# Attention in a two-layer backbone: two of five key blocks are split in two parts by POOL from an SBUF copy, three by DVE from PSUM

## The chip, the cores and the metric

One core of one Trainium2 chip runs the whole program in one launch. The metric is the device time of an execution in microseconds, the median of the runs shown. TensorE is called PE here (PEld is its weight load), VectorE DVE, ScalarE ACT, GpSimd POOL and SyncE SP.

## What is computed

The program is a two-layer backbone over 1024 latent tokens and 256 context tokens, width 1024. Layer 0 mixes with grouped-query attention (12 query heads, 4 key heads, head size 64) beside a convolution, layer 1 with a long convolution beside a recurrence; each layer ends in a gated feed-forward block. The change lies in the attention of layer 0 alone:

```python
def block_attention(q, k, v):                       # per block of 128 queries
    s = jnp.einsum('bqhgd,bkhd->bhgqk', q_blk, k)   # scores
    p = jax.nn.softmax(s, axis=-1)
    return jnp.einsum('bhgqk,bkhd->bqhgd', p, v)
# latent queries see 256 context keys and 1024 latent keys; context queries see the 256 context keys
```

## The kernel before

**Units.** `attention_all` (L875) walks 60 units. A latent unit is one head and 256 latent queries against all 1280 keys; there are 48 (4 key heads, 3 query heads each, 4 times 256 queries). A context unit is one head and the 256 context queries against 256 keys; there are 12. Each unit has two halves of 128 queries.

**Scores.** `score_steps` (L998) multiplies queries by keys into the one PSUM tile `S`, which holds both halves (L1008, L1009: two matmuls per piece, because the keys lie there in two parts). For each half DVE finds the negated row maximum `nm` (L1025) and ACT writes the exponentials `p` to SBUF and their sum `sm` (L1026).

**Values.** `value_steps` (L1030) turns the exponentials round. For each block of 256 keys, five per latent unit (`b` from 0 to 4) and one per context unit, PE makes four 128x128 transposes into a PSUM tile `pT` of 128x512 (L1048). There are two buffers for it (`npt=2`), and the transposes `zT` of the next head's queries and keys (L993) use the same two. The matmul with the values takes each factor as a sum of two parts of a shorter type: ACT rounds `pT` to the high part `ph` (L1052), DVE subtracts, `pl = pT - ph` (L1053), and both stay in SBUF. The buffer of `pT` is free when DVE has read it. The matmuls that add `ph` and `pl` into the PSUM tile `o` (L1059) are put off by `DELAY = 2` blocks (`late`). At a unit's end ACT copies one half of `o` to `bot` (L1067), DVE adds it and multiplies by the reciprocal sum (two instructions `ot`, by the helper `add`, L1188), and SP stores `ot`. `o` has one buffer, so the next unit's first matmul into it waits for the second `ot`.

**Beside it.** Two side streams are fed in. `stack_gen` (L960) prepares the next key head: POOL and ACT split queries and keys in two parts `zst` (L981 to L986), in batches of two or four tiles, PE transposes them, ACT copies the results. `load_early` (L825) reads finished pieces of the attention output back from DRAM as `ysrc` (two buffers), and POOL splits them, `och` (L833) and `ocl` (L834 by the helper). Near the end POOL also splits the first weights of the next stage, `wlo` (L332).

**Order.** The order on each engine comes from a scheduler, which sorts by the priority of the program's order and by its own estimate of when an instruction is ready. On the chip each engine then runs its list strictly in that order, and waits where an operand is not there.

Of the kernel before, what the change touches and what calls it, by code (L numbers as in the profile page):

```python
# [10 lines left out]
F32 = mybir.dt.float32  # L11
F32R = mybir.dt.float32r
AF = mybir.ActivationFunctionType
ALU = mybir.AluOpType
# [3 lines left out]
P = 128  # L18
# [229 lines left out]
class Kern:  # L248
# [781 lines left out]
    def value_steps(self, u, state):  # L1030

        nc = self.nc
        ab = self.ab
        nk, r, oq, h0 = u
        vs = self.gr[h0 // 3][3]
        ob = self.pa.tile([P, 512], F32, name="o", tag="o", bufs=1)
        o = ob[:, :256]
        nb = nk // 256
        rs = ab.tile([P, 2], F32, name="rs", tag="rs", bufs=2)
        nc.vector.reciprocal(out=rs, in_=state["sm"])  # L1040
        for b in range(nb):
            pt = self.pa.tile([P, 512], F32, name="pT", tag="pt", bufs=self.npt)
            for a in range(2):
                for i, p in enumerate(state["p"]):
                    kc = 2 * b + a
                    if nb > 1 and i == 0:
                        kc = (kc - 2) % NT
                    nc.tensor.transpose(pt[:, (2 * a + i) * P:(2 * a + i + 1) * P], p[:, kc * P:(kc + 1) * P],  # L1048
                                        self.ident)
            ph = ab.tile([P, 512], F32R, name="ph", tag="ph", bufs=4)  # L1050
            pl = self.st.tile([P, 512], F32R, name="pl", tag="sq", bufs=3)
            nc.scalar.copy(ph, pt)  # L1052
            nc.vector.tensor_tensor(out=pl, in0=pt, in1=ph.bitcast(F32), op=ALU.subtract)  # L1053

            def then(b=b, ph=ph, pl=pl):
                for a in range(2):
                    kc = 2 * b + a
                    for j, x in enumerate((ph, pl)):
                        nc.tensor.matmul(o, lhsT=vs[:, kc], rhs=x[:, a * 256:a * 256 + 256],  # L1059
                                         start=(kc == 0 and j == 0), stop=(kc == nk // P - 1 and j == 1))  # L1060
                if b < nb - 1:
                    return
                bot, ot = (ab.tile([64, 256], F32, name=m, tag=m, bufs=n) for m, n in (("bot", 1), ("ot", 2)))
                rt = ob[:64, 256:512]
                for i in range(2):
                    nc.tensor.transpose(rt[:, i * P:(i + 1) * P], rs[:, i:i + 1].to_broadcast([P, 64]), self.ident)
                nc.scalar.copy(bot, o[64:128])  # L1067
                self.add(ot, o[0:64], bot)
                self.add(ot, rt, ot, ALU.mult)
                h = h0 + r  # L1070
                nc.sync.dma_start(out=self.od[h // 2][(h % 2) * 64:(h % 2) * 64 + 64, oq:oq + 256], in_=ot)
            self.late.append(then)
            if len(self.late) > self.DELAY:
                self.late.pop(0)()
            yield
# [874 lines left out]
```

## Time and profile before

| | |
|---|---|
| runs | 3852.33, 3854.68, 3864.87 us; median 3854.68 |
| profiled execution | 3860.75 us, its span 3858.7 us, so 2.05 us lie around the span |
| PE busy | 3516.5 us, 91% of the span |
| DVE, ACT, POOL busy | 2289.8 (59%), 1248.0 (32%), 1334.2 us (35%) |
| attention | some 418 to 1001 us of the span |

The span runs from the first to the last instruction. "Busy" counts instructions in progress; a matmul's end is modelled, and consecutive ones overlap. A group of instructions is one line of code on one engine with one shape: its count, total and mean time, and the idle time of the engine just before them with what ended it. The chain that ended last is followed back from the end of a window, at each step to what released an instruction or to the one before it on its engine; "issue" in it is time in which the engine waited for nothing that the profile shows.

### The profile page before, as it was taken

What the parts mean: (1) busy time and instruction counts of PE and PEld (TensorE: products, weight loads), DVE (VectorE), ACT (ScalarE), POOL (GpSimd) and SP (SyncE); (2) the same over time, 40 slices, a digit from 0 to 9 for tenths busy, and PEclk for the clock granted to TensorE, in tenths of its full rate; (3) what the DMA queues carried; (4) which work ended last, traced back from release to release, by engine and by line L of the source; (5) the groups of instructions that cost most, each with busy time, mean ns of one, the idle gap of its engine ahead of it and who ended that gap; (6) DMA issues with size and microseconds to landing.
All of it is one profiled execution on the core that took longest, in us unless ns stands there. A gap on an engine that the chain in (4) does not pass through costs nothing.

```text
span 3858.7 us, 47940 instructions
## 1 busy us (share of the span) xinstructions
PE 3516.5 (91%) x18708; PEld 2924.3 (76%) x18708; DVE 2289.8 (59%) x2847; ACT 1248.0 (32%) x2123; POOL 1334.2 (35%) x1003
## 2 busy tenths in 40 slices
PE   7988688888899999999999899999878899999998
PEld 4768466776687888888888778977666778888886
DVE  5977456666326666655555689455698554343435
ACT  4135566666333211122222422222112342222222
POOL 3248331100152111123333554355566642222223
PEclk9999789999999999999999899999898999999999
DMA  5376111000223223212222367433345311111111
GB/s 204 118 189 142 59 60 33 21 19 25 101 71 99 77 93 106 73 54 72 81 77 72 120 199 208 140 98 96 117 147 195 129 58 49 45 48 50 44 50 55
DMA packets 204017, 356.39 MB, mean 92 GB/s; under 512 B 23632, under 2 KB 124560, under 8 KB 203792
## 3 DMA queue, kind: packets, MB, share of 16 engines
q1 hardware_dynamic: 172240, 311.22, 24.8%
q0 software_dynamic: 27648, 35.76, 4.4%
q10 hardware_dynamic: 3904, 6.36, 0.5%
q8 instruction: 148, 2.42, 0.3%
q14 instruction: 77, 0.63, 0.1%
HBM read 275.04 MB, written 62.39 MB: 87 GB/s over the span
## 4 chain that ended last, share of the span: by engine, by line
PE 65%; DVE 12%; issue 4%; ACT 3%; DMA 3%; POOL 1%; SPq 0%; POOLq 0%; ACTq 0%; DVEq 0%
PE dl L338 13%; PE dl L339 13%; PE dl L340 13%; PE pj L338 2%; PE pT L1048 2%; PE pj L339 2%; PE pj L340 2%; DVE nm L1025 2%; PE o L1059 2%; DVE pl L1053 2%; PE S L1008 1%; PE dc L338 1%; PE dc L340 1%; PE dc L339 1%; PE S L1009 1%
## 5 line engine op out<-in xcount | busy, mean ns | idle before, releaser
L332 POOL TENSOR_TENSOR wlo<-wraw,whi 128x1024 fp32r<-128x1024 f32 (+1 forms) x226 | 567.4, 2516 | 1289.0 <-ACT whi L331 1288.8
L339 PE MATMUL dl<-hl,whi 128*128 128x512 f32 x1920 | 763.2, 398 | 3.8 <-POOL hl L1188 2.9
L338 PE MATMUL dl<-hh,whi 128*128 128x512 f32 x1536 | 607.0, 396 | 11.9 <-DVE fc L1099 8.7
L340 PE MATMUL dl<-hh,wlo 128*128 128x512 f32 x1536 | 607.9, 396 | 0.0
L331 ACT CAST whi<-wraw 128x1024 fp32r<-128x1024 f32 (+1 forms) x226 | 225.1, 1005 | 887.3 <-PE dl L339 415.2
L339 PEld LDWEIGHTS dl<-hl,whi 128*128 128x128 f32 x1920 | 362.9, 189 | 88.2 <-POOL hl L1188 4.6
L338 PEld LDWEIGHTS dl<-hh,whi 128*128 128x128 f32 x1536 | 289.3, 188 | 80.7 <-issue 7.0
L1097 DVE SCALAR_TENSOR_TENSOR fc<-dl,cols,fc 128x1023 f32<-128x1023 f32 x84 | 107.4, 1279 | 408.6 <-ACT fc L1096 408.6
L340 PEld LDWEIGHTS dl<-hh,wlo 128*128 128x128 f32 x1536 | 289.3, 188 | 68.7
L872 DVE SCALAR_TENSOR_TENSOR x<-dl,modT,x 128x1024 f32<-128x1024 f32 x160 | 204.1, 1277 | 113.7 <-PE dl L340 112.2
L338 PE MATMUL dl<-gs,whi 128*128 128x512 f32 x640 | 253.2, 396 | 9.1 <-DVE fc L1099 9.1
L339 PE MATMUL dl<-gs,whi 128*128 128x512 f32 x640 | 250.2, 391 | 0.0
L340 PE MATMUL dl<-gs,wlo 128*128 128x512 f32 x640 | 250.0, 391 | 0.0
L1053 DVE TENSOR_TENSOR pl<-pT,ph 128x512 fp32r<-128x512 f32 x252 | 167.5, 685 | 65.9 <-ACT ph L1052 65.3
L1048 PE MATMUL pT<-ident,p 128*128 128x128 f32 x1008 | 166.8, 288 | 41.6 <-DVE pl L1053 34.5
L1052 ACT CAST ph<-pT 128x512 fp32r<-128x512 f32 x252 | 142.7, 587 | 153.5 <-PE pT L1048 152.2
L1025 DVE TENSOR_REDUCE nm<-S 128x1 f32<-128x1280 f32 (+1 forms) x120 | 153.0, 1275 | 51.5 <-PE S L1009 47.1
L1059 PE MATMUL o<-ph,vs 128*128 128x256 f32 x504 | 147.0, 305 | 36.9 <-ACT ph L1052 18.9
L1048 PEld LDWEIGHTS pT<-ident,p 128*128 128x128 f32 x1008 | 121.5, 146 | 64.4 <-DVE pl L1053 48.4
L1192 DVE SCALAR_TENSOR_TENSOR conv<-u,cols,conv 128x1287 f32<-128x1287 f32 (+14 forms) x96 | 160.4, 1698 | 0.9
L338 PE MATMUL dl<-hl,whi 128*128 128x512 f32 x384 | 155.0, 405 | 1.7 <-ACT whi L331 0.8
L1059 PE MATMUL o<-pl,vs 128*128 128x256 f32 x504 | 152.3, 325 | 2.2 <-DVE pl L1053 2.2
(373 smaller groups left out, 8390.9 us busy)
## 6 DMA issues: line engine op xcount, KB each, us to landing
wraw<-in_wup SPq DMA_DIRECT2D x88, 512.0 KB, 3.5
adaw<-in_adaw SPq DMA_DIRECT2D x128, 256.0 KB, 2.8
wraw<-in_wdn SPq DMA_DIRECT2D x44, 512.0 KB, 3.5
adaw<-in_adaw SPq DMA_DIRECT2D x32, 512.0 KB, 4.1
df<-in_dftf POOLq DMA_DIRECT2D x64, 256.0 KB, 3.8
wraw<-in_w1f SPq DMA_DIRECT2D x24, 512.0 KB, 3.7
x<-in_xT SPq DMA_DIRECT2D x16, 640.0 KB, 10.1
spd<-so SPq DMA_DIRECT2D x68, 128.0 KB, 2.2
```

Source lines behind the costliest of these rows:

```text
L331: nc.scalar.copy(hi[:, :cols], raw[:, :cols])
L332: nc.gpsimd.tensor_tensor(out=lo[:, :cols], in0=raw[:, :cols], in1=hi[:, :cols].bitcast(F32), op=ALU.subtract)
L338: mm(out, lhsT=lh, rhs=rh, start=first, stop=False)
L339: mm(out, lhsT=lh, rhs=rl, start=False, stop=False)
L340: mm(out, lhsT=ll, rhs=rh, start=False, stop=last)
L872: nc.vector.scalar_tensor_tensor(out=xl, in0=pl, scalar=self.mod(l, j, m, 0), in1=xl, op0=ALU.mult, op1=ALU.add)
L1025: nc.vector.tensor_reduce(out=nm[:, i:i + 1], in_=s, op=ALU.max, axis=AX.X, negate=True)
L1048: nc.tensor.transpose(pt[:, (2 * a + i) * P:(2 * a + i + 1) * P], p[:, kc * P:(kc + 1) * P], self.ident)
L1052: nc.scalar.copy(ph, pt)
L1053: nc.vector.tensor_tensor(out=pl, in0=pt, in1=ph.bitcast(F32), op=ALU.subtract)
L1059: nc.tensor.matmul(o, lhsT=vs[:, kc], rhs=x[:, a * 256:a * 256 + 256], start=(kc == 0 and j == 0), stop=(kc == nk // P - 1 and j == 1))
L1192: self.nc.vector.scalar_tensor_tensor(out=out, in0=a, scalar=s, in1=b, op0=ALU.mult, op1=op)
```

## The change

For the odd blocks (`b` is 1 and 3; a context unit has only `b` = 0) ACT copies `pT` unrounded to a new SBUF tile `pf` of 128x512, which has one buffer. POOL then rounds `pf` to `ph` and subtracts to get `pl`. The even blocks stay as they were. The values that reach the matmuls are the same.

```diff
             ph = ab.tile([P, 512], F32R, name="ph", tag="ph", bufs=4)
             pl = self.st.tile([P, 512], F32R, name="pl", tag="sq", bufs=3)
-            nc.scalar.copy(ph, pt)
-            nc.vector.tensor_tensor(out=pl, in0=pt, in1=ph.bitcast(F32), op=ALU.subtract)
+            if b % 2:
+                pf = ab.tile([P, 512], F32, name="pf", tag="pf", bufs=1)
+                nc.scalar.copy(pf, pt)
+                nc.gpsimd.tensor_copy(ph, pf)
+                self.add(pl, pf, ph.bitcast(F32), ALU.subtract, pool=True)
+            else:
+                nc.scalar.copy(ph, pt)
+                nc.vector.tensor_tensor(out=pl, in0=pt, in1=ph.bitcast(F32), op=ALU.subtract)
```

Six lines are added, so lines behind it move: L1052 and L1053 become L1058 and L1059 for the even blocks, L1054 is the copy to `pf`, L1055 POOL's rounding; L1059 becomes L1065, L1067 becomes L1073, and the helper's L1188 becomes L1194. 96 blocks of 252 take the new way. The scheduler makes a new order for the attention; outside it the order stays the same but for a few instructions at its end.

DVE in the steady part late in the attention, one latent unit, first before and then with the change (`nm` is the row maximum, `pl` the subtraction, `ot` the unit's result, `rs` the reciprocal):

```order
L1025 TENSOR_REDUCE nm<-S 128x1
L1053 TENSOR_TENSOR pl<-pT,ph 128x512 x4
L1025 TENSOR_REDUCE nm<-S 128x1
L1053 TENSOR_TENSOR pl<-pT,ph 128x512
L1040 RECIPROCAL rs<-sm 128x2
L1188 TENSOR_TENSOR ot<-o,bot 64x256
L1188 TENSOR_TENSOR ot<-o,ot 64x256
L1025 TENSOR_REDUCE nm<-S 128x1
```

```order
L1025 TENSOR_REDUCE nm<-S 128x1
L1059 TENSOR_TENSOR pl<-pT,ph 128x512
L1194 TENSOR_TENSOR ot<-o,bot 64x256
L1059 TENSOR_TENSOR pl<-pT,ph 128x512
L1194 TENSOR_TENSOR ot<-o,ot 64x256
L1025 TENSOR_REDUCE nm<-S 128x1
L1059 TENSOR_TENSOR pl<-pT,ph 128x512
L1040 RECIPROCAL rs<-sm 128x2
L1025 TENSOR_REDUCE nm<-S 128x1
```

Of the five `pl` of a unit three stay, and the two `ot` have come to stand ahead of the unit's second `nm`.

ACT in the same part, from one exponential `p` to the one after the next, before and with the change:

```order
L1026 ACTIVATE p,sm<-S,nm 128x1280
L1052 CAST ph<-pT 128x512 x3
L1026 ACTIVATE p,sm<-S,nm 128x1280
L1067 COPY bot<-o 64x256
L1052 CAST ph<-pT 128x512 x2
L1026 ACTIVATE p,sm<-S,nm 128x1280
```

```order
L1026 ACTIVATE p,sm<-S,nm 128x1280
L1073 COPY bot<-o 64x256
L1058 CAST ph<-pT 128x512
L1054 COPY pf<-pT 128x512
L1058 CAST ph<-pT 128x512
L1026 ACTIVATE p,sm<-S,nm 128x1280
```

Two of ACT's five copies write `pf` in place of `ph`. The copy `bot` now stands ahead of three copies between two exponentials.

POOL in the first third of the attention, where `load_early` splits its first pieces, before and with the change:

```order
L833 CAST och_1_5260<-ysrc 128x256 x3
L833 CAST och_1_5277<-ysrc 128x256 x2
L1188 TENSOR_TENSOR ocl_1_5261<-ysrc,och_1_5260 128x256 x3
L1188 TENSOR_TENSOR ocl_1_5278<-ysrc,och_1_5277 128x256 x2
L833 CAST och_2_5262<-ysrc 128x256 x3
L833 CAST och_2_5279<-ysrc 128x256 x2
L1188 TENSOR_TENSOR ocl_2_5263<-ysrc,och_2_5262 128x256 x3
L1188 TENSOR_TENSOR ocl_2_5280<-ysrc,och_2_5279 128x256 x2
```

```order
L1055 CAST ph<-pf 128x512
L833 CAST och_1_5308<-ysrc 128x256 x3
L1194 TENSOR_TENSOR pl<-pf,ph 128x512
L833 CAST och_1_5325<-ysrc 128x256 x2
L1194 TENSOR_TENSOR ocl_1_5309<-ysrc,och_1_5308 128x256 x3
L1055 CAST ph<-pf 128x512
L1194 TENSOR_TENSOR ocl_1_5326<-ysrc,och_1_5325 128x256 x2
L1194 TENSOR_TENSOR pl<-pf,ph 128x512
L833 CAST och_2_5310<-ysrc 128x256 x3
L833 CAST och_2_5327<-ysrc 128x256 x2
L1055 CAST ph<-pf 128x512
L1194 TENSOR_TENSOR ocl_2_5311<-ysrc,och_2_5310 128x256 x3
```

The roundings `ph` and subtractions `pl` stand among the pieces `och` and `ocl`, up to five of them between the `ph` and the `pl` of one block.

## Rows read from the trace of the kernel before

**Rows 1.** Busy time per engine in three windows, in us: PE, PEld, DVE, ACT, POOL, clock, DMA
```profile
420.00:1000.00 580.00, 467.58 (x2968) 390.91 (x2968) 377.66 (x572) 359.51 (x658) 91.81 (x165) 0.94 0.10 30
540.00:580.00 40.00, 33.60 (x235) 28.73 (x235) 27.85 (x43) 26.00 (x52) 23.92 (x48) 1.00 0.18 58
820.00:860.00 40.00, 32.97 (x226) 27.78 (x227) 28.26 (x43) 25.30 (x46) 0.00 (x0) 1.00 0.03 8
```

**Rows 2.** Chain that ended last, 420 to 1000 us, shares by engine and line
```profile
by line: PE pT L1048 12.0%; DVE nm L1025 11.5%; PE o L1059 11.3%; issue 10.7%; DVE pl L1053 10.6%; PE S L1008 9.7%; PE S L1009 8.3%; ACT p L1026 5.9%; ACT ph L1052 5.7%; DVE ot L1188 2.2%; PE zT L993 1.7%; PE o L1066 1.4%; PE mu L849 1.2%; 
```

**Rows 3.** Groups on DVE, 420 to 1000 us: shapes, count, busy us, mean ns, idle before
```profile
L1053 DVE TENSOR_TENSOR pl<-pT,ph 128x512 fp32r<-128x512 f32 x252 | 167.5, 685 | 65.9 <-ACT ph L1052 65.3
L1025 DVE TENSOR_REDUCE nm<-S 128x1 f32<-128x1280 f32 x95 | 141.5, 1490 | 45.5 <-PE S L1009 44.4
...
L1188 DVE TENSOR_TENSOR ot<-o,ot 64x256 f32<-64x256 f32 x59 | 24.4, 413 | 1.6
```

**Rows 4.** Groups on ACT, 420 to 1000 us
```profile
L1052 ACT CAST ph<-pT 128x512 fp32r<-128x512 f32 x252 | 142.7, 587 | 153.5 <-PE pT L1048 152.2 <-ACT nt L861 0.4 <-DVE nm L1025 0.3
...
L1067 ACT COPY bot<-o 64x256 f32<-64x256 f32 x59 | 21.8, 369 | 25.3 <-PE o L1066 22.5
```

**Rows 5.** Waits, 420 to 1000 us: who for whom, us in total, times, longest
```profile
PE pT L1048 <- DVE pl L1053: 34.5, 56, 1.7
```

**Rows 6.** Timeline of DVE, 906 to 917 us: start, length, what, idle before
```profile
906.61 1.49 DVE L1025 TENSOR_REDUCE nm<-S 128x1 f32<-128x1280 f32 x1 [0.37 <-PE S L1009]
908.01 1.28 DVE L1053 TENSOR_TENSOR pl<-pT,ph 128x512 fp32r<-128x512 f32 x2
910.12 0.69 DVE L1053 TENSOR_TENSOR pl<-pT,ph 128x512 fp32r<-128x512 f32 x1 [0.82 <-ACT ph L1052]
911.02 0.69 DVE L1053 TENSOR_TENSOR pl<-pT,ph 128x512 fp32r<-128x512 f32 x1 [0.21 <-ACT ph L1052]
911.63 1.49 DVE L1025 TENSOR_REDUCE nm<-S 128x1 f32<-128x1280 f32 x1
...
916.35 1.49 DVE L1025 TENSOR_REDUCE nm<-S 128x1 f32<-128x1280 f32 x1 [0.36 <-PE S L1009]
```

**Rows 7.** Timeline of ACT, 906 to 911 us
```profile
906.99 1.07 ACT L1052 CAST ph<-pT 128x512 fp32r<-128x512 f32 x2 [1.65 <-PE pT L1048]
908.13 1.33 ACT L1026 ACTIVATE p<-S,nm 128x1280 f32<-128x1280 f32 x1
...
909.50 0.59 ACT L1052 CAST ph<-pT 128x512 fp32r<-128x512 f32 x1
910.40 0.59 ACT L1052 CAST ph<-pT 128x512 fp32r<-128x512 f32 x1 [0.32 <-PE pT L1048]
```

**Rows 8.** Groups on POOL, 420 to 1000 us
```profile
L1188 POOL TENSOR_TENSOR ocl<-ysrc,och 128x256 fp32r<-128x256 f32 x35 | 24.7, 740 | 0.0
L984 POOL TENSOR_TENSOR zst<-zl,zst 128x192 fp32r<-128x192 f32 x26 | 15.3, 600 | 0.0
L833 POOL CAST och<-ysrc 128x256 fp32r<-128x256 f32 x35 | 12.7, 403 | 110.0 <-DMA ysrc<-od 103.0 <-issue 7.0
L986 POOL TENSOR_TENSOR zst<-zl,zst 128x128 fp32r<-128x128 f32 x26 | 11.4, 461 | 0.0
L981 POOL CAST zst<-zl 128x192 fp32r<-128x192 f32 x26 | 8.0, 348 | 94.9 <-PE zT L993 65.0 <-issue 29.9
L332 POOL TENSOR_TENSOR wlo<-wraw,whi 128x1024 fp32r<-128x1024 f32 x3 | 7.1, 2368 | 79.0 <-ACT whi L331 79.0
L1188 POOL TENSOR_TENSOR acc<-acc,sq 128x512 f32<-128x512 f32 x4 | 5.1, 1274 | 54.6 <-ACT sq L435 54.5
...
L974 POOL CAST vs<-p 128x640 fp32r<-128x640 f32 x3 | 2.2, 719 | 8.2 <-DMA p<-zd 7.4 <-PE zT L993 0.8
```

**Rows 9.** Group on DVE, 540 to 580 us
```profile
L1053 DVE TENSOR_TENSOR pl<-pT,ph 128x512 fp32r<-128x512 f32 x21 | 13.8, 684 | 4.8 <-ACT ph L1052 4.8
```

**Rows 10.** The same group, 820 to 860 us
```profile
L1053 DVE TENSOR_TENSOR pl<-pT,ph 128x512 fp32r<-128x512 f32 x21 | 14.0, 686 | 4.7 <-ACT ph L1052 4.6
```

## The prediction, made before the changed kernel was run

> **What bounds the kernel now.** I read the busy times of the attention first. From 420 to 1000 us PE is in progress 468 of 580 us, DVE 378, ACT 360 and POOL 92 [rows 1]. No engine is full, and POOL is nearly idle. So the stage is bound by a loop that runs through several engines, and the chain of waits says which. It spends 10.6% in `pl` on DVE, 11.5% in `nm` on DVE, 5.7% in `ph` on ACT, and most of the rest in PE's matmuls [rows 2]. The waits agree: PE stood 34.5 us before transposes because DVE had not yet read a `pT` buffer [rows 5].
>
> Then I looked for the loop in one latent unit. From one first row maximum to the next, 906.61 to 916.35, it takes 9.74 us [rows 6]. The first `nm` starts at 906.61, the second at 911.63, 5.02 us later. In between DVE ran four `pl`, and before two of them it stood 0.82 and 0.21 us, because ACT had put the 1.33 us exponential between its copies [rows 6, 7]. From the second `nm` to the next unit's first `nm` it takes the other 4.72 us: maximum, exponential, scores. A unit gets shorter by what the 5.02 us lose, since the 4.72 us hold no `pl` that counts (the one after 911.63 runs beside the exponential).
>
> **The change part by part.** *DVE loses 96 `pl`* of 0.685 us [rows 3], 66 us of busy time. This is not the gain; the gain is what leaves the loop.
>
> *The loop after the change.* By the new order of DVE and ACT (shown above), between the two `nm` stand `pl`, `ot`, `pl`, `ot`, and ACT runs exponential, `bot`, `ph`. The path is: `nm` to exponential 1.52 (908.13 less 906.61); exponential to the next ACT instruction 1.37 (909.50 less 908.13) [rows 6, 7]; `bot` 0.37 [rows 4]; `ph` 0.59, then 0.03 to `pl` (911.02 less 910.40 and 0.59); `pl` to the next DVE instruction 0.61 (911.63 less 911.02) [rows 6, 7]; `ot` 0.41 [rows 3]. That is 4.90 us. Consecutive instructions overlap by some 0.10: two casts took 1.07 us, where twice 0.587 is 1.17 [rows 4, 7]. Taken off for `bot` and `ot` it gives 4.70. So a unit loses between 0.12 and 0.32 us of 9.74. I take 0.32, because the rows show the overlap, and **48 latent units give 15 us**. Bounds: nothing, if other waits fill it, and 25 us, if two fifths of all `pl` on the chain vanish (0.4 of 10.6% of 580 us [rows 2]). The earlier release of `pT` by ACT is part of this and is not counted again.
>
> *ACT's copy to `pf`* has the shape and source of the cast that it replaces, 0.587 us [rows 4]: nothing, with `ph` on either side of zero by far less than the other terms.
>
> *POOL gains 96 casts and 96 subtractions* of 128x512. The subtraction is bounded by the add of the same shape, 1.274 us; the cast lies between 128x256 with 0.403 and 128x640 with 0.719, so 0.61 [rows 8]. A pair takes 1.88 us, all together 181 us on an engine with 92 of 580 us used [rows 1]. On average this is hidden: pairs come every 4.9 us (two per unit), `pf` is held for 0.59 + 1.88 = 2.47 us, and the matmuls on it are put off by two blocks. So a pair may be 2.4 us late at no cost. What happens beyond: the next copy to `pf` waits for POOL on ACT, behind it stand a `ph` and the exponential, and PE's scores wait for that. The cover is gone where POOL has other work in its list.
>
> *Where POOL has other work.* The worst place is the first third of the attention, between two batches of `zst`. There POOL has 23 `och` (23 x 0.403 = 9.3 us), 23 `ocl` (23 x 0.740 = 17.0), two batches of four `zst` (8 x (0.348 + 0.461 + 0.600) = 11.3) [rows 8], and in the new order 7 pairs (13.2): **50.8 us of work while attention advances by 3.5 units**. These take 34 us at 9.74 and 42 us at the stage's mean of 12.1 (580 by 48); I take 37 as nearer to the steady rows. 50.8 - 37 - 2.4 leaves 11; since the second batch can spread beyond the place, I count **10 us lost**, between 0 and 17. `och` also waits for DMAs, 103 us in all before [rows 8], where it cost nothing because POOL had nothing else to do; SP's list, which stores `ot` and loads `ysrc` in order, sets these times, and a pair behind such a wait is late with it. This is within the bound.
>
> *The other batches.* Six batches of `zst`, the 12 later `och` with their `ocl`, and three `wlo` of 2.37 us [rows 8] stand between pairs too. A batch and a pair are 5.6 + 1.9 = 7.5 us against 4.9 + 2.4 = 7.3, so about 0.5 us each: **4 us** for the eight places, between 0 and 20 (2.5 us each, if none finds slack).
>
> *DVE and POOL at the same time.* With POOL busy 23.9 of 40 us a `pl` took 684 ns, with POOL idle 686 ns [rows 1, 9, 10], so I add nothing. The Trainium skill speaks against such a move: in "Perfetto Trace Analysis", section Optimizing Scalar/DVE Operations, it says that DVE and POOL share a port, "so offloading operations between those two might not help". In "SBUF — State Buffer", section Who interferes with whom, it narrows this to DVE instructions with two inputs in SBUF (or in certain fast modes); `pl` has one input in PSUM. By the narrow rule the sum stays; by the broad one it would be the last rival below.
>
> **The sum.** 15 off, 10 and 4 on: 1 us faster, no change that can be measured. Against the profiled execution that is 3859.7 instead of 3860.75 us. This execution lies 6.07 us above the median of the runs, which is 3854.68, so the forecast is **3854 us**. What counts as no change is 0.3%, 11.6 us, about what a measurement of this kernel can tell.
>
> **Rivals.** *A: the chain loses its `pl` fully and POOL's lateness is absorbed.* The loop then gains the 25 us of the upper bound, and only some 4 us come back: 21 us faster, 3834 us. For it: `pl` is on the chain throughout [rows 2], and in the new order PE's matmuls stand further behind their transposes, so a late pair is met later. Against it: what holds the second `nm` in rows 6 is as much ACT's order as DVE's.
>
> *B: POOL's list becomes the bound.* One `pf` and one in-order list tie ACT to POOL; wherever POOL has over 2.4 us of other work between two pairs, the copy to `pf` and with it the exponential wait. With the loop gaining only half (7 us), the first third costing its 17 and the other places 15, it is 25 us slower, 3880 us. For it: up to five pieces stand between the `ph` and `pl` of one block in the new order, and the sum of 50.8 us is firm in its parts. Against it: POOL is free of other work after the first weights, and the steady part has slack. It decides where the pairs' lateness exceeds 2.4 us.
>
> *C: DVE and POOL shut each other out.* DVE's steps are about a quarter of the chain (`nm`, `pl` and `ot` [rows 2]); 181 us of new POOL work that holds them up costs 0.25 x 181 = 45, less the 15: 30 us slower, 3885 us. Against it: rows 9 and 10. This is the broad rule quoted above.
>
> *D: it does nothing*, 3855 us: the loop holds elsewhere and POOL hides all.
>
> **How the numbers follow.** Forecast 0.40, A 0.30, B 0.24, C 0.04, D 0.02. Of the forecast, its own spread puts 0.05 beyond 11.6 us on the fast side and 0.03 on the slow side; of A 0.27 and of B 0.20 lie beyond. Faster: 0.05 + 0.27 = 0.32. Slower: 0.03 + 0.20 + 0.04 = 0.27. No change: 0.41. The bounds of the sum are 25 faster and 37 slower; the range leaves a tenth on each side and goes from 3829 to 3880. The forecast's own range is 3843 to 3866.
>
> **What would show it.** DVE's `pl` falls to 156 of 685 ns; POOL shows 96 casts near 0.61 us and 96 subtractions near 1.27 us. Right is the forecast if a steady unit late in the attention takes about 9.4 us and the part with the first 23 `och` takes longer per unit, with ACT waiting for POOL before `pf`. A is right if that part takes no longer per unit than before; B if waits of ACT or PE for POOL also lie outside it; C if a DVE instruction's duration grows while POOL works. The prediction is wrong in its mechanism if the steady unit's time does not fall at all, or if the time moves outside the attention.

## The result, and the profile after

| | before | after |
|---|---|---|
| runs shown, median | 3856.36 us (3852.33 to 3864.87, 4 runs) | 3881.76 us (3875.92 to 3891.32, 4 runs) |
| ratio, 95% interval | | 1.0058 [1.0039, 1.0076] |
| profiled execution | 3860.75 us | 3891.32 us, span 3889.6 us |

The changed kernel is 0.58% slower, some 22 us (the two medians differ by 25.4). The forecast of 3854 us was wrong, and the time lies just beyond the range's end at 3880 us. The profiled execution is the slowest of the four, 9.6 us above the median, so of its own lengths only differences inside the attention are used below.

First the busy times of the attention after the change, with the columns of [rows 1]:

```profile
420.00:1000.00 580.00, 454.87 (x2829) 384.34 (x2828) 303.54 (x456) 342.83 (x630) 263.44 (x346) 0.90 0.10 30
500.00:540.00 40.00, 27.20 (x141) 22.67 (x141) 14.84 (x22) 23.82 (x40) 23.85 (x41) 0.74 0.24 77
540.00:580.00 40.00, 27.56 (x141) 23.37 (x141) 13.99 (x22) 16.81 (x35) 26.16 (x47) 0.73 0.18 50
740.00:780.00 40.00, 28.83 (x151) 25.30 (x150) 16.06 (x23) 17.48 (x33) 20.65 (x28) 0.74 0.12 33
```

DVE is relieved as planned (304 us for 378), and POOL rises from 92 to 263 us. But from 540 to 580 us PE gets through 141 matmuls where it ran 235 [rows 1], at a granted clock of 0.73 for 1.00, and 740 to 780 us looks the same.

The groups on DVE, ACT and POOL, 420 to 1030 us (the same stage, which now ends later):

```profile
L1059 DVE TENSOR_TENSOR pl<-pT,ph 128x512 fp32r<-128x512 f32 x156 | 105.7, 685 | 44.7 <-ACT ph L1058 43.9
L1054 ACT COPY pf<-pT 128x512 f32<-128x512 f32 x96 | 56.3, 587 | 23.6 <-PE pT L1048 17.2 <-POOL pl L1194 5.4
L1194 POOL TENSOR_TENSOR pl<-pf,ph 128x512 fp32r<-128x512 f32 x96 | 124.4, 1296 | 13.5 <-POOL ph L1055 6.0 <-PE o L1065 2.0
L1055 POOL CAST ph<-pf 128x512 fp32r<-128x512 f32 x96 | 58.8, 613 | 257.6 <-ACT pf L1054 223.8 <-DVE nm L1025 16.0 <-PE o L1065 13.6
L833 POOL CAST och<-ysrc 128x256 fp32r<-128x256 f32 x35 | 12.9, 401 | 23.6 <-DMA ysrc<-od 23.6
```

Every price is as the prediction took it: 0.685, 0.587, 1.296 and 0.613 us (estimated 1.274 and 0.61 for the last two). A `pl` on DVE takes what it took before, with POOL now busy beside it. POOL stands 224 us idle before its casts, waiting for ACT's copies, so over the whole stage POOL has time to spare.

The waits, 420 to 1030 us (who for whom, us in total, times, longest):

```profile
DVE nm L1025 <- PE S L1009: 111.0, 60, 5.6
PE S L1008 <- ACT p L1026: 62.7, 74, 3.9
ACT p L1026 <- PE pT L1048: 31.1, 16, 4.7
...
ACT pf L1054 <- POOL pl L1194: 5.4, 6, 1.3
PE o L1065 <- POOL pl L1194: 4.8, 4, 2.9
...
PE o L1065 <- POOL ph L1055: 3.6, 2, 1.9
```

and the first three of them in the kernel before, same window:

```profile
DVE nm L1025 <- PE S L1009: 47.1, 50, 2.8
...
PE S L1008 <- ACT p L1026: 23.8, 26, 3.4
...
ACT p L1026 <- PE pT L1048: 5.1, 3, 4.8
```

The waits of ACT and PE that name POOL are 13.8 us together (PE's weight loads for the same matmuls name it for 10.6, DVE for 2.4). The large growth is elsewhere: DVE waits 64 us more for scores, PE 39 us more for exponentials. The score loop runs slower without POOL's name on it.

**Where it happens.** Each unit begins its values with one reciprocal `rs` on DVE (L1040), so the timeline of DVE dates the 60 units. The table gives the start of `rs` in the kernel before, and how much later or earlier it is in the others (us, one profiled execution each; all but before and after are explained below):

| unit | before | after | e1 | e2 | e3 | e4 | e7 | e8 | e11 | e14 |
|---|---|---|---|---|---|---|---|---|---|---|
| 0 | 425.4 | -1.2 | +0.3 | -0.1 | +2.6 | +1.6 | +1.1 | -0.9 | +2.7 | -1.1 |
| 6 | 505.8 | -7.5 | -4.1 | -4.5 | -3.3 | +1.8 | -3.3 | +1.7 | -1.8 | -7.4 |
| 12 | 572.0 | +14.7 | +14.2 | +16.9 | -3.9 | +20.0 | -2.3 | +2.2 | +17.1 | +6.1 |
| 28 | 714.6 | +18.5 | +18.5 | +17.4 | -3.9 | +25.3 | -4.2 | +2.2 | +19.4 | +8.6 |
| 32 | 750.5 | +31.0 | +21.5 | +14.9 | -6.0 | +33.7 | -6.7 | +2.2 | +23.7 | +11.7 |
| 59 | 993.0 | +24.0 | +10.1 | +5.0 | -12.2 | +29.0 | -14.6 | +2.2 | +14.6 | +4.1 |

Read the third column downwards. The change **gains 6.3 us in units 0 to 6, loses 22.2 in units 6 to 12, loses 12.5 in units 28 to 32**, loses another 3.8 between these two places, and gains again to the end. At the two losing places POOL splits finished pieces (`och`, `ocl`) between its pairs. The profiled executions differ by 30.9 us in their spans, and 24.0 at unit 59, so 6.9 us lie behind the start of unit 59. The profiled executions of the other runs differ there from the kernel before by up to 8 us, in either direction, and no run explains it.

### The profile page after: what moved, and what is told of

It is laid out like the page before. It is cut to its first block, busy times and chain, and to the rows that moved or that the text cites. A ratio compares the mean times of both kernels' runs of the same rounds, so it can differ in the third digit from the quotient of the medians.

```text
span 3889.6 us, 48162 instructions
## 1 busy us (share of the span) xinstructions
PE 3524.4 (91%) x18708; PEld 2933.6 (75%) x18708; DVE 2222.8 (57%) x2751; ACT 1247.0 (32%) x2121; POOL 1524.7 (39%) x1195
## 4 chain that ended last, share of the span: by engine, by line
PE 65%; DVE 10%; ACT 5%; issue 5%; POOL 3%; DMA 2%; SPq 0%; POOLq 0%; DVEq 0%; ACTq 0%
PE dl L338 13%; PE dl L339 13%; PE dl L340 13%; ACT p L1026 2%; PE pj L338 2%; PE pj L339 2%; PE pj L340 2%; PE S L1008 2%; PE o L1065 1%; PE dc L338 1%; PE dc L339 1%; PE dc L340 1%; PE pT L1048 1%; PE S L1009 1%; PE Bp L1571 1%
## 5 line engine op out<-in xcount | busy, mean ns | idle before, releaser
L332 POOL TENSOR_TENSOR wlo<-wraw,whi 128x1024 fp32r<-128x1024 f32 (+1 forms) x226 | 576.2, 2555 | 1214.8 <-ACT whi L331 1210.5
L338 PE MATMUL dl<-hh,whi 128*128 128x512 f32 x1536 | 607.6, 397 | 11.9 <-DVE fc L1105 8.7
L1008 PE MATMUL S<-k,q 128*128 128x512 f32 (+1 forms) x312 | 126.9, 414 | 66.3 <-ACT p L1026 66.0
L1065 PE MATMUL o<-ph,vs 128*128 128x256 f32 x504 | 146.4, 312 | 19.7 <-DVE ot L1194 14.0
L1026 ACT ACTIVATE p<-S,nm 128x1280 f32<-128x1280 f32 (+1 forms) x120 | 139.0, 1159 | 68.3 <-DVE nm L1025 34.9
L1055 POOL CAST ph<-pf 128x512 fp32r<-128x512 f32 x96 | 58.8, 613 | 257.6 <-ACT pf L1054 223.8
```

What stands on the lines that cost most here:

```text
L332: nc.gpsimd.tensor_tensor(out=lo[:, :cols], in0=raw[:, :cols], in1=hi[:, :cols].bitcast(F32), op=ALU.subtract)
L338: mm(out, lhsT=lh, rhs=rh, start=first, stop=False)
L1008: nc.tensor.matmul(S[:, dst:dst + n], lhsT=a, rhs=k1[:, key:key + n], start=True, stop=False)
L1026: nc.scalar.activation(p, s, AF.Exp, bias=nm[:, i:i + 1], accum_out=sm[:, i:i + 1])
```

## The experiments

Theory H was at first: the loss is POOL's pairs standing late behind pieces, above all behind pieces that wait for their loads. Rival S: the single `pf` buffer ties ACT to POOL everywhere. The first four runs shared their runs of the kernel before (median 3861.97 us).

**e1, two buffers of `pf`.**

```diff
-                pf = ab.tile([P, 512], F32, name="pf", tag="pf", bufs=1)
+                pf = ab.tile([P, 512], F32, name="pf", tag="pf", bufs=2)
```

> The changed kernel with two buffers for pf instead of one. Theory H (a pair's pl stands in POOL's list behind och, which waits for its DMA, or behind a pile of och and ocl; PE and ACT stall for it and PE then runs at its lower clock): the second buffer frees ACT's copy but not pl, so at most 5 us come back of the 25 us lost against before; about 3877 us. Rival S (the single pf buffer is what ties ACT to POOL): most of the loss of the first third and of the place near 740 us comes back, 15 us or more, to 3866 us or less.

Measured: 3865.61 us (3860.94 to 3871.58, 12 runs), ratio 1.0008 [0.9997, 1.002]. Most of the loss is gone, more than H allowed. The table shows that S is right at one place only: units 28 to 32 lose 3.0 us instead of 12.5, but units 6 to 12 still lose 18.3 of 22.2. Moreover the second buffer changes the order that the scheduler writes, so e1 is not a clean test of the buffer alone.

**e2, the pieces' loads read an input and not the stored attention output**, so no load waits for a store; the pieces hold other values.

```diff
-                self.nc.sync.dma_start(out=y, in_=src[:, a:b])
+                self.nc.sync.dma_start(out=y, in_=self.i["xT"][0][:, a:b])
```

> The changed kernel, but load_early reads its pieces from an input in DRAM instead of the attention output that was stored shortly before, so a load no longer waits for a store; the split pieces then hold other values, same sizes and same work. POOL's work stays whole, only its waits for the DMA of ysrc (23.6 us in the changed kernel) should mostly go. Theory H in its form 'the wait for the DMA': 15 us or more come back, about 3865 us. Theory H in its form 'the pile of work': at most 5 us come back, about 3878 us, and the first third still takes as long.

Measured: 3869.25 us (3860.22 to 3878.73, 12 runs), ratio 1.0014 [1.0003, 1.0025]. The total looks like support for H, and the trace takes the support away. Units 6 to 12 still lose 21.4 us. With the dependence gone, the scheduler moved the later pieces forward too, so none stand at units 28 to 32, and that loss is gone with them. And `och` still waits for its loads in units 6 to 12, though less (9.5 us in the whole attention, for 23.6). The timeline of POOL in e2:

```profile
546.14 1.08 POOL L833 CAST och<-ysrc 128x256 fp32r<-128x256 f32 x3 [4.58 <-DMA ysrc<-in_xT]
```

What holds the load up is partly SP's list. The buffer for the wait of 4.58 us came free with the end of an `ocl` at 540.3. SP issued the load 2.4 us later, right behind a store of `ot`; POOL had then waited for 1.1 of its 4.58 us. SP's timeline in e2, and then the waits of its queue, 515 to 570 us:

```profile
542.12 0.45 SPq L1077 DMA_DIRECT2D od<-ot  x1
542.67 0.53 SPq L830 DMA_DIRECT2D ysrc<-in_xT  x1
```
```profile
SPq L1077 <- DVE ot L1194: 24.4, 4, 11.0
```

SP stood up to 11.0 us at a store of `ot` (L1077), and a load (L830) behind it on SP's list comes after it. So e2 told only that the loss at units 28 to 32 goes where the pieces go.

**e3 and e4, pairs on POOL in some units only.** e3 keeps them out of units 6 to 35, where pieces stand; e4 has them only there. (`un` counts the units.)

```diff
-            if b % 2:
+            if b % 2 and not 6 <= un < 36:
```

In e4 the condition is `6 <= un < 36`.

> POOL takes the odd blocks only in units 0 to 5 and 36 to 59, where the new order of the changed kernel has no och or ocl; in units 6 to 35 DVE splits all blocks as before (48 of the 96 pairs stay on POOL). Theory H: the gains that the changed kernel shows in these units stay (about 7 us in the first, 5 us in the last) and the loss goes: 10 to 12 us faster than before, about 3845 us. Rival G (a pair on POOL costs wherever it stands): slower than before by about half of the changed kernel's loss, 12 us.

> The complement: POOL takes the odd blocks only in units 6 to 35, where och and ocl stand in its list. Theory H: the whole loss stays and the gains go, 30 to 38 us slower than before, about 3890 us. Rival G: slower by about half of the changed kernel's loss, 12 us, like e3_outside.

Measured: e3 3841.01 us (3835.35 to 3844.43, 6 runs), ratio **0.9944 [0.993, 0.9959]**; e4 3886.54 us (3877.69 to 3898.75, 6 runs), ratio 1.0068 [1.0049, 1.0087]. e3 beats both kernels, and the kernel before by more than expected (21 us for 10 to 12); the whole loss lies in the units of e4. In e3 the clock of the critical stretch is back; its busy times from 540 to 580 us, with the columns of [rows 1]:

```profile
540.00:580.00 40.00, 32.31 (x223) 27.22 (x222) 27.25 (x43) 25.34 (x51) 22.62 (x45) 1.00 0.17 52
```

**e7 and e8, the pieces' work left out**, in the changed kernel (e7) and in the kernel before (e8). This separates pieces from units, which e3 could not.

```diff
-                y = self.ysrc(pool)[:, :b - a]
-                self.nc.sync.dma_start(out=y, in_=src[:, a:b])
-                for e in range(a, b, 256):
...
-                    yield 0.7
+                for e in (hi, lo):
+                    self.nc.sync.dma_start(out=e[:, a:b].bitcast(F32), in_=src[:, a:b])
+                yield 0.7 * (b - a) / 256
```

> The changed kernel, with POOL's work on the finished pieces left out: each piece is loaded straight into both part tiles, so the parts hold plain copies and not a split, and POOL's list in units 7 to 13 and 28 to 31 holds pairs and zst alone. To be compared with the kernel before under the same edit (e8). Theory L (the loss comes where pieces and pairs share POOL's in-order list; a pair alone costs nothing and a latent unit gains 0.26 us): e7 is 10 to 20 us shorter than e8, and the lag of units 6 to 12 and 30 to 32 against e8 is gone. Theory T (one pf buffer ties ACT to POOL at every pair, which is what e1 took away): the tie remains, e7 is no shorter than e8 or up to 10 us longer.

> The kernel before, with the same work left out: the finished pieces are loaded straight into both part tiles. Theory L: the 49 us of POOL work on pieces were hidden in the kernel before, so this run stands within 5 us of it. A third view, P (the pieces cost the kernel before something too, since POOL's list is late there as well): 5 to 15 us shorter than before.

Measured, beside a kernel before of 3861.25 us: e7 3845.21 us (3838.49 to 3852.64, 6 runs), ratio **0.9959 [0.9946, 0.9972]**; e8 3861.2 us (3854.15 to 3870.75, 11 runs), ratio 1.0004 [0.9992, 1.0016]. Theory L stands. Without pieces the change is worth 16 us (3861.2 less 3845.21), with them it costs 22; so pairs and pieces together cost about 38 us that neither costs alone (26 to 50 by the two intervals). Rival T falls: the single buffer is still there in e7. So does P, since the pieces cost the kernel before nothing. The edit takes away the pieces' work, their waits and their places in POOL's list at once, and the scheduler writes new lists for the other engines too, so it does not say which of these costs the time.

The maxima show the difference. DVE's wait for scores from 515 to 595 us, in turn before, after and e7:

```profile
DVE nm L1025 <- PE S L1009: 5.0, 6, 1.6
```
```profile
DVE nm L1025 <- PE S L1009: 35.9, 11, 5.6
```
```profile
DVE nm L1021 <- PE S L1005: 11.2, 9, 3.5
```

After less e7 is 24.7 us, about the loss of units 6 to 12.

**e9 and e10, only the two places left to DVE.** e9 keeps pairs off POOL in units 6 to 15 and 28 to 33 alone; e10 also has two `pf` buffers (the edit of e1).

```diff
-            if b % 2:
+            if b % 2 and not (6 <= un < 16 or 28 <= un < 34):
```

> POOL makes the pairs of all units but 6 to 15 and 28 to 33, where the finished pieces stand in its list; there DVE splits as before. Theory L: the 13 more latent units than in e3 add their steady gain of 0.26 us each, so 3 us less than e3's 3841: 3836 to 3840. Theory T: the units 16 to 27 run with the single buffer beside the zst batches of two heads and lose there, 3843 to 3855.

> As e9, with two buffers of pf. Theory L: within 3 us of e9, since a second buffer mends only what the pieces hold up. Theory T: 5 to 15 us shorter than e9.

Measured: e9 3848.08 us (3841.4 to 3852.22, 6 runs), ratio 0.9961 [0.9947, 0.9974]; e10 3842.51 us (3834.36 to 3859.63, 6 runs), ratio 0.9951 [0.9933, 0.997]. Both beat both kernels, but e9 is a miss for L: 8 us above the upper end of what was expected, and not below e3. It lies in T's range, and e10 at the near end of T's, 5.6 us below e9 with intervals that overlap. The trace of e9, dated like the table, shows why the 13 more units brought nothing: its lag against before is -3.6 us at unit 16, -7.1 at unit 22, and -3.0 again at unit 28. What the pairs gain there they lose again in two intervals, 3.3 us from unit 22 to 23 and 3.7 from 26 to 27, with a batch of `zst` on POOL at the first and just before the second; in e3, where DVE makes these pairs, both lose 0.0. In e10 the lag goes from -10.4 to -7.3 us over these units, so a second buffer does not mend it.

**e11, the pieces' loads issued by POOL** and not behind SP's stores. Theory W: the waiting loads cause the loss; theory V: the pieces' own work does.

```diff
-                self.nc.sync.dma_start(out=y, in_=src[:, a:b])
+                self.nc.gpsimd.dma_start(out=y, in_=src[:, a:b])
```

> The changed kernel, with the loads of the finished pieces issued by POOL itself and not by SP, where they stood behind the stores of ot. Theory W (POOL's pairs are late because a piece in front of them waits for a load that SP holds behind a store): the idle time of och falls from 23.6 to under 8 us and the loss of 22 us at units 6 to 12 to under 10; 3855 to 3870. Theory V (the pieces' own work is too much there: with the loads in time the loss stays): within 6 us of the changed kernel, 3876 to 3888.

Measured, beside 3860.1 us: 3872.33 us (3862.57 to 3879.9, 10 runs), ratio 1.003 [1.0019, 1.0042]. Between the two, and the trace says why (the order of the pieces shifts a little with the edit). The group of `och`, 420 to 1030 us:

```profile
L833 POOL CAST och<-ysrc 128x256 fp32r<-128x256 f32 x35 | 12.7, 401 | 4.5 <-DMA ysrc<-od 4.2 <-DVE pl L1059 0.3
```

The waits for loads are nearly gone (4.2 us for 23.6). Units 28 to 32 then lose 4.3 us and not 12.5, as W has it, and units 6 to 12 still 18.9 of 22.2, as V has it.

**e14 and e15, both steps of the pieces moved to DVE**, e15 with two `pf` buffers as well.

```diff
-                    self.nc.gpsimd.tensor_copy(hi[:, e:e + 256], ye)
-                    self.add(lo[:, e:e + 256], ye, hi[:, e:e + 256].bitcast(F32), ALU.subtract, pool=True)
+                    self.nc.vector.tensor_copy(hi[:, e:e + 256], ye)
+                    self.add(lo[:, e:e + 256], ye, hi[:, e:e + 256].bitcast(F32), ALU.subtract)
```

> The whole change, with both steps of the finished pieces moved from POOL to DVE, so that POOL holds pairs, zst and a few others alone. Theory L: as with the pieces left out (e7, 16 us below the kernel before), less what 46 times two short steps on DVE cost, some 26 us of work for an engine that the change relieved of some 66: 3843 to 3853. Rival D (the pieces' waits for their loads then stand in DVE's list ahead of the maxima and the other blocks): 3860 to 3880.

> As e14, with two buffers of pf. Theory L: within 5 us of e14, 3838 to 3853. If the single buffer ties ACT to POOL in the steady units too: 5 to 15 us below e14.

Measured: e14 3868.02 us (3859.19 to 3881.52, 11 runs), ratio 1.0023 [1.0012, 1.0035]; e15 3862.97 us (3859.95 to 3870.52, 11 runs), ratio 1.0008 [0.9997, 1.0019]. Rival D: DVE's groups in e14 show the pieces' waits on the engine that has the maxima.

```profile
L833 DVE CAST och<-ysrc 128x256 fp32r<-128x256 f32 x35 | 11.7, 379 | 11.9 <-DMA ysrc<-od 11.9
```

Units 6 to 12 lose 13.5 us. DVE stands 11.9 us before the pieces; that this is what costs the 13.5, as D has it, is not shown. Both runs miss L's range. e15 lies 5.1 us below e14 with intervals that overlap, so it decides nothing about the buffer.

**How late a pair is.** Pairing each `pf` copy on ACT with its `pl` on POOL by order, the time from the end of the first to the end of the second is at least 2.02 us in each run below. Its mean over the pairs begun from 515 to 595 us: after 4.21 us (10 pairs), e11 4.11 (10), e14 2.53 (12), e7 2.40 (14). So it separates after and e11 from e7, but not e14, whose units 6 to 12 lose 13.5 us with pairs about as prompt as in e7. One slow pair of the changed kernel: ACT ends the copy at 545.78 and POOL ends the `pl` at 552.08, with five `ocl` in between. First ACT's timeline, then POOL's:

```profile
545.20 0.58 ACT L1054 COPY pf<-pT 128x512 f32<-128x512 f32 x1
```
```profile
543.70 1.09 POOL L833 CAST och<-ysrc 128x256 fp32r<-128x256 f32 x3 [4.77 <-DMA ysrc<-od]
546.08 0.75 POOL L833 CAST och<-ysrc 128x256 fp32r<-128x256 f32 x2 [1.30 <-DMA ysrc<-od]
546.78 0.62 POOL L1055 CAST ph<-pf 128x512 fp32r<-128x512 f32 x1
547.35 3.48 POOL L1194 TENSOR_TENSOR ocl<-ysrc,och 128x256 fp32r<-128x256 f32 x5
550.78 1.30 POOL L1194 TENSOR_TENSOR pl<-pf,ph 128x512 fp32r<-128x512 f32 x1
```

## Why the prediction was wrong

**The step that failed is "Where POOL has other work", with "The other batches" behind it.** It put the first third at 10 us, between 0 and 17, and the other places at 4. Measured: units 6 to 12 lose 22.2 us in the table, units 28 to 32 another 12.5, and pairs and pieces together cost 38 (e7, e8), where the sum had 14. Three things in the step were off. The term for the loop was mis-sized too, as told under what was luck.

*The method.* I compared POOL's total work with the time of 3.5 units and granted 2.4 us of slack for each pair. In the first place POOL was not even full: 50 of 80 us from 500 to 580. Nor were the pairs much later than the sum allowed: 4.21 us in the mean, for the 1.88 of a pair and the 2.4 called free, though five of the ten took some 4.9 to 6.5. What grew there is the loop of scores, maximum and exponential (DVE's wait for scores, 35.9 us for 5.0), and the step had no term for it. e1 and e11 show that neither a second buffer nor loads in time mends units 6 to 12.

*The later pieces.* Units 28 to 32 were within the "other batches" at half a microsecond each; they lost 12.5. There one pair's wait can be seen whole. POOL's timeline of the changed kernel, then PE's:

```profile
736.15 0.61 POOL L1055 CAST ph<-pf 128x512 fp32r<-128x512 f32 x1 [5.49 <-ACT pf L1054]
741.05 0.75 POOL L833 CAST och<-ysrc 128x256 fp32r<-128x256 f32 x2 [4.28 <-DMA ysrc<-od]
741.76 1.26 POOL L1194 TENSOR_TENSOR pl<-pf,ph 128x512 fp32r<-128x512 f32 x1
```
```profile
743.08 0.58 PE L1065 MATMUL o<-pl,vs 128*128 128x256 f32 x1 [2.86 <-POOL pl L1194]
```

The `ph` of a block was ready at 736.76. Its `pl` stood behind two `och`, those behind a load, and PE stood 2.86 us for `pl`. The prediction named this ("a pair behind such a wait is late with it") and then called it "within the bound". For the first third it was not: 22.2 us for 17. For the later places it was, 12.5 of up to 20 for eight of them, but the sum had counted 4.

*The clock.* The prediction had no term for PE's granted clock. The busy times before that stall, after it and later:

```profile
732.00:742.00 10.00, 7.46 (x52) 6.15 (x50) 6.20 (x10) 5.41 (x11) 1.56 (x4) 1.00 0.16 42
743.00:756.00 13.00, 10.74 (x40) 9.54 (x41) 4.18 (x4) 4.84 (x8) 6.29 (x11) 0.50 0.03 13
757.00:770.00 13.00, 9.86 (x74) 8.72 (x73) 7.50 (x12) 7.39 (x14) 7.15 (x7) 0.99 0.19 43
```

Within the stall the clock fell to 0.50 (from 742.5 us on), the lower level of 1.2 GHz, and PE ran 13 us at it, busy for 10.74 of them. What this cost in all is not known, since no run has the pairs' waits without it.

**What was right, and what was luck.** *The loop's gain* came out near by luck. 15 us less 4 for the other batches was forecast, and e8 less e7 is 16, but the working does not hold in its parts. A steady unit late in the attention was to take about 9.4 us. DVE's timeline of the changed kernel, four lines in between left out:

```profile
936.44 1.49 DVE L1025 TENSOR_REDUCE nm<-S 128x1 f32<-128x1280 f32 x1 [0.95 <-PE S L1009]
940.42 0.69 DVE L1059 TENSOR_TENSOR pl<-pT,ph 128x512 fp32r<-128x512 f32 x1 [0.20 <-ACT ph L1058]
941.03 0.41 DVE L1194 TENSOR_TENSOR ot<-o,ot 64x256 f32<-64x256 f32 x1
941.36 1.47 DVE L1025 TENSOR_REDUCE nm<-S 128x1 f32<-128x1280 f32 x1
946.04 1.49 DVE L1025 TENSOR_REDUCE nm<-S 128x1 f32<-128x1280 f32 x1 [1.56 <-PE S L1009]
```

It takes 9.60 us (936.44 to 946.04) for 9.74 before. The second `nm` comes 4.92 us after the first: that is the path's 4.90 without the overlap of 0.20 that the prediction took off. So a steady unit gains 0.14 us and not 0.32, and 48 of them would give 7 us. The rest of e7's gain against e8 lies where the working had none: 5.5 us between units 1 and 2, 0.85 from unit 51 to the context unit 52, 1.9 between the two units behind it, and the like at others. The other batches do cost: in e7 the interval from unit 26 to 27, just after a batch of `zst`, is 2.7 us longer than in e8, and that from 46 to 47, beside the three `wlo`, 3.7, where half a microsecond was counted for each. The fall of the changed kernel's lag from 31.2 us at unit 34 to 25.7 at unit 58 (0.29 us for each of 19 latent units) is a mean of all this, and does not bear out the 0.32. *The prices* of the new instructions were right. *No contention*: 685 ns per `pl`. The total is what the Trainium skill would have one expect ("Perfetto Trace Analysis", Optimizing Scalar/DVE Operations: offloading between the two "might not help"), but this trace does not show its reason; in e3 and e7 the same offloading helped.

**The rivals.** B came nearest: 3880 us forecast, by one in-order list that ties ACT to POOL, where pairs have other work between them. Its place was right and its total nearly so, but by other parts: its 7 us for the loop is what steady units give, while the whole gain without pieces was 16, and the places cost 38 for B's 32. POOL does have over 2.4 us of other work between pairs at both places, but B's path through the single `pf` does not carry the first: with the second buffer of e1 the units 6 to 12 lose nearly as much. A, C and D fall: no steady unit gains what A has, a `pl` on DVE takes what it took (C), and the time changed (D).

**What stays open.** How a lateness of 1.8 us on ten pairs becomes 22 us in units 6 to 12 is not shown. Direct waits for POOL are only 2.1 us of PE's time there:

```profile
PE o L1065 <- POOL ph L1055: 1.7, 1, 1.7
...
PE o L1065 <- POOL pl L1194: 0.4, 1, 0.4
```

Two things could carry the rest: the lists of ACT, PE and DVE, which the scheduler lays out by its own estimate of when a pair is ready, and the granted clock (0.73 there, 1.00 before). Both differ between after and e7, and no run changed one without the other. The traces lean to the lists. In units 6 to 12 DVE's list of the changed kernel has two maxima in a row, with no `pl` between, at three points; one of them, and then DVE at the same unit in e7 (its two `ot` behind the `pl` left out):

```profile
564.91 1.49 DVE L1025 TENSOR_REDUCE nm<-S 128x1 f32<-128x1280 f32 x1 [5.58 <-PE S L1009]
569.24 0.43 DVE L1025 TENSOR_REDUCE nm<-S 128x1 f32<-128x256 f32 x1 [2.84 <-PE S L1009]
569.58 1.28 DVE L1059 TENSOR_TENSOR pl<-pT,ph 128x512 fp32r<-128x512 f32 x2
```
```profile
553.24 1.49 DVE L1021 TENSOR_REDUCE nm<-S 128x1 f32<-128x1280 f32 x1
554.64 0.68 DVE L1055 TENSOR_TENSOR pl<-pT,ph 128x512 fp32r<-128x512 f32 x1
558.31 1.49 DVE L1021 TENSOR_REDUCE nm<-S 128x1 f32<-128x1280 f32 x1
```

In the first, two `pl` stand behind two waits for scores, 8.4 us together. Such doubled maxima stand in units 6 to 12 of every run that loses there (after 3, e1 4, e2 3, e4 2, e11 2, e14 and e15 1; losses of 11.1 to 22.2 us) and of none that does not (before, e3, e7 to e10; a gain of 3.0 to a loss of 1.0). They do not set the size, and elsewhere they can be cheap: units 28 to 32 of e1 have two and lose 3.0 us, as e14 does with none. The clock follows the loss less well: e1 loses 18.3 us at 0.91 from 540 to 580 us. This is a comparison of traces; no run forced the old order on DVE.

## What to carry to other kernels

Before work goes to an idle engine, look in its list for instructions that were allowed to be late, here 35 `och` that waited 103 us for loads at no cost [rows 8]: once an urgent instruction stands behind them, their waits can become its waits, as at 741 us. Adding up the engine's work did not price such a place; the loss came with 50 of 80 us busy. Read the new lists of all engines at such places too, and not only in the steady part: a doubled maximum on DVE went with the loss of units 6 to 12. And move the work where the list is free: the same change limited to the units outside (e3) gave 0.56%, where all of them lost 0.58%.

## What was not expected of the hardware

In a stall of 2.86 us in front of one matmul the granted clock fell, and the 13 us from 743 to 756 us ran at 0.50. Over 540 to 580 us the clock was 0.73 in the changed kernel, 1.00 in the kernel before [rows 1] and 1.00 in e3. And a DMA load can be late for a reason that is not its own: in e2 it depended on nothing but its buffer, and was issued 2.4 us after that came free, behind a store on SP's list; 1.1 of the 4.58 us that POOL waited for it went by so.
